# Attention's q, k and v transfers in 8-block transposes and one store of v per 512 tokens

## The chip, the cores and the metric

The kernel runs on one core of one Trainium2 chip. The metric is the device time of one execution in microseconds (us), as the median of three runs.

## The reference

One decoder layer over 2048 tokens of width 1024, with 8 heads of 64. One projection makes six streams; a gated short convolution and dilated attention run side by side on them; their outputs are normed, projected and added to x; a gated feed-forward part follows.

```python
h = rms_norm(x, g_mix[l])
z = h @ w_in[l]
u, gb, gc, q, k, v = jnp.split(z, splits, axis=-1)
y_conv = gb * short_conv(gc * u, conv_w[l])
q = rms_norm(q.reshape(B, S, N_HEADS, HEAD_DIM), g_q[l]) * (HEAD_DIM ** -0.5)
k = rms_norm(k.reshape(B, S, N_HEADS, HEAD_DIM), g_k[l])
v = v.reshape(B, S, N_HEADS, HEAD_DIM)
y_attn = dilated_mixture(q, k, v).reshape(B, S, D_ATTN)
mix = jnp.concatenate([rms_norm(y_conv, g_conv_out[l]), rms_norm(y_attn, g_attn_out[l])], axis=-1)
x = x + mix @ w_out[l]
h = rms_norm(x, g_ffn[l])
x = x + (jax.nn.silu(h @ w_gate[l]) * (h @ w_up[l])) @ w_down[l]
```

`dilated_mixture` lets every head attend in three branches of (window, dilation): (128, 1), (512, 4) and (2048, 16). In each, a query sees at most 129 keys at the branch's stride; the branches are summed with weights from their softmax denominators. Attention has no other positions.

## The kernel before

Products keep nearly full precision by splitting each operand in two halves of float16 (`h` and `l`) and adding three matmuls (L187 to L189).

**Stages.** `in_and_conv` norms x (`norm`, L251: 16 tiles of 128 tokens, each turned by two transposes into `self.x`), splits and spills the weights, and runs three of four convolution blocks (`conv_steps`). `attention_pairs` makes q, k and v of the first head pair alone (`qkv_steps(0)`). Then, for each of the four pairs `g`, the steps of `attn_steps(g)` alternate with steps of a filler: `qkv_steps(g + 1)` while there is a next pair, then `tail_steps` (the last convolution block and `out_a`, the first half of the output projection). `out_b` and `ffn` follow.

**What sets the order.** The code is recorded in program order, and a scheduler then orders every engine's instructions by its own estimate of when each is ready. Only edges like `issue_after` (L713) bind it. On the chip each engine runs its list in order: what waits holds up all that stands behind it. All large DMAs and all transposes stand in one such list, SyncE's (SP).

**`qkv_steps`** goes through the 2048 tokens in four steps of 512. In each, four matmul groups (128 tokens, 384 columns: q and k of two heads, v of two heads) are read out. v goes as two halves into `vs`, and is stored to DRAM (`d_v`, L466) after the second and the fourth group, for each head apart. DVE and POOL norm q and k. ACT and POOL then split them into `qkhl` (q of head 0 and 1 as halves, k's upper half twice) and `klz` (k's lower half beside zeros), L483 to L486. Six transposes of 4 blocks of 128 x 128 follow (L489 to L494): two into `qp`, two into `ka`, two into `kb` (called `kl` in the code). Two copies on DVE (L496) put `qp` into `qT` in token order.

**`attn_steps`** runs, for each of a pair's two heads, the branches in the order 1, 2, 0 (numbered from 0 as listed above): load v for the branch (`load_v`), score matmuls into `s` (L597, L598), DVE's mask and row minimum (L603), ACT's exponential (L608). Where the blocks have earlier keys, ACT and DVE make the halves `eh` (L618, L619; four buffers) and one transpose of 8 blocks turns them into `et` (L620). Where they have none (branch 2, and the first step of branch 1), the result goes to `sm` and TensorE transposes it (L613). Then come the AV matmuls into `av` (L626), and ACT copies `av` out (L629).

**Tiles.** The pool `qk` has three names, `qT`, `ka` and `kb`, with four buffers of 4 KB each per partition. They serve attention's `qT`, `ka` and `kl` (two buffers each for the two heads of a pair), and also the norm's halves, the convolution's `cu` and `w2`, and the tiles `ya`, `t`, `x1` and `xn` of the output projection. A tile takes whichever buffer of its name the scheduler finds free.

Of the kernel before, what the change touches and what calls it, by code (L numbers as in the profile page):

```python
# [8 lines left out]
F32 = mybir.dt.float32  # L9
# [8 lines left out]
P = 128  # L18
S = 2048
# [10 lines left out]
class Builder:  # L30
# [237 lines left out]
    def conv_steps(self, j, W, before=None, scratch=None):  # L268
# [3 lines left out]
        NC = 512  # L272
        prev = None
        for c in range(S // NC):
            if before:
# [20 lines left out]
            ups, u = yield from gemm(0)  # L296
            cu = own[:, 4:6].rearrange("p a b -> p (a b)") if own is not None else self.qk.tile([P, D], F32, name="ka")
            if c == 0:
# [9 lines left out]
            gb, u = yield from gemm(1)  # L308
            w2 = own[:, 2:4] if own is not None else self.qk.tile([P, 2, NC], F32, name="kb")
            y, s2 = w2[:, 0], w2[:, 1]  # L310
# [45 lines left out]
    def in_and_conv(self):  # L356
        tc, nc, A = self.tc, self.nc, self.A
        w_in, w_out = A["w_in"][0], A["w_out"][0]
        with ExitStack() as c:
# [23 lines left out]
            def norm(i, n):  # L383
                tags = 6 * ("nx_x",) + ("qT", "qT") + 8 * ("nx_x",)
                self.norm(i, [(self.qk if tg != "nx_x" else xp).tile([P, D], F32, name=tg) for tg in tags[i:i + n]],
                          [self.qk.tile([P, 2, D], F16, name=tg) for tg in ("ka", "ka", "ka", "qT")[i % 4:i % 4 + n]])
            spills = []
# [45 lines left out]
    def qkv_steps(self, g, st):  # L433
# [8 lines left out]
        qT = [self.qk.tile([P, S], F16, name="qT") for _ in range(2)]  # L442
        ka = [self.qk.tile([P, S], F16, name="ka") for _ in range(2)]
        kl = [self.qk.tile([P, S], F16, name="kb") for _ in range(2)]
        dv = self.d_v[g]
        for i in range(0, NT, 4):
            f = self.at.tile([P, 4, 4, HD], F32, name="qkf", bufs=2)
            for j in range(4):
                vs = self.vs[j // 2]

                t = slice(j, 4 * P, 4)
                xh, xl = self.x[i // 4]
                ps = self.psmm.tile([P, 512], F32, name="mm")
                yield from self.mm3_steps(ps[:, 0:384], lambda k: xh[:, k, t], lambda k: xl[:, k, t],
                                          lambda k: wh[:, k], lambda k: wl[:, k])
                if j == 0:
                    n = self.at.tile([P, 16, HD], F32, name="qkn")
                nc.scalar.activation(f[:, j].rearrange("p a b -> p (a b)"), ps[:, 0:256], AF.Copy, scale=u)
                nc.scalar.activation(n[:, 4 * j:4 * j + 4].rearrange("p a b -> p (a b)"), ps[:, 0:256], AF.Square, scale=u)
                pv = ps[:, 256:384].rearrange("p (h d) -> p h d", h=2)  # L460
                vh, vl = (vs[:, j % 2, :, x, 0:HD] for x in range(2))
                nc.scalar.activation(vh, pv, AF.Copy, scale=2.0 ** -20)
                nc.vector.scalar_tensor_tensor(vl, pv, 2.0 ** -20, vh, op0=ALU.mult, op1=ALU.subtract)  # L463
                if j % 2 == 1:
                    for h in range(2):
                        nc.sync.dma_start(dv[h, i * P:(i + 4) * P].rearrange("(p t) c -> p t c", t=4)[:, j - 1:j + 1],  # L466
                                          vs[:, :, h].rearrange("p t x d -> p t (x d)"))
            ff = f.rearrange("p a b d -> p (a b) d")
# [10 lines left out]

            hl = self.at.tile([P, 4, 4, 2, HD], F16, name="qkhl")  # L480
            for h in range(2):
                q, k = n4[:, :, h], n4[:, :, 2 + h]
                nc.scalar.copy(hl[:, h, :, 0], q)  # L483
                nc.scalar.copy(hl[:, 2 + h], k.unsqueeze(2).broadcast_to([P, 4, 2, HD]))
                nc.gpsimd.tensor_tensor(hl[:, h, :, 1], q, hl[:, h, :, 0], op=ALU.subtract)
                nc.gpsimd.tensor_tensor(self.klz[:, h, :, 0], k, hl[:, 2 + h, :, 0], op=ALU.subtract)  # L486


            four = [self.at.tile([P, 4, P], F16, name="qp", bufs=4) for _ in range(2)]  # L489
            for src, dsts in ((hl, (*four, *ka)), (self.klz, kl)):  # L490
                for n_, dst in enumerate(dsts):
                    self.transpose(dst if n_ < 2 and src is hl else
                                   dst[:, i * P:(i + 4) * P].rearrange("p (j t) -> p j t", j=4),
                                   src[:, n_].rearrange("p j x d -> p (j x d)"))  # L494
            for h in range(2):
                nc.vector.tensor_copy(qT[h][:, i * P:(i + 4) * P].rearrange("p (t j) -> p t j", j=4),  # L496
                                      four[h].rearrange("p j t -> p t j"))
            yield
        st.update(qT=qT, ka=ka, kl=kl)

    def attn_steps(self, g, st):
# [18 lines left out]
        for h, b in [(h, b) for h in range(2) for b in (1, 2, 0)]:  # L520
            qT, ka, kl = (st[x][h] for x in ("qT", "ka", "kl"))
            load_v(h, b)
# [39 lines left out]
            def keys(tl, u, prev):  # L562

                k = tl.rearrange("p (n j t) -> p n j t", n=4, j=4)
                n = u // 4
                if b == 0:
                    m = u % 4
                    k = k.rearrange("p n j (m t) -> p n m j t", m=4)
                    if prev and m == 0:
                        return [k[:, n - 1, 3], k[:, n, 0]]  # L570
                    return [k[:, n, m - prev:m + 1]]
                if b == 1:
                    return [k[:, n - prev:n + 1, u % 4]]
                return [k[:, :, u % 4, u // 4::4]]
# [5 lines left out]
            for u0 in (0, 8, 4, 12) if last and b == 0 else range(0, NT, 4):  # L580
# [3 lines left out]
                for us in (range(u0, u0 + 4),) if four else (range(u0, u0 + 2), range(u0 + 2, u0 + 4)):  # L584
# [14 lines left out]

                    sm = self.ep.tile([P, 512], F32, name="sm") if four else sp  # L600

# [56 lines left out]
    def attention_pairs(self):  # L658
# [29 lines left out]

        self.klz = self.at.tile([P, 2, 4, 2, HD], F16, name="klz")
        nc.gpsimd.memset(self.klz, 0.0)  # L690
        self.y7 = self.rows.tile([P, NT, HD], F32, name="y7")

        self.vs = [self.at.tile([P, 2, 2, 2, HD + 1], F16, name=f"vs{i}") for i in range(2)]
        for t in self.vs:
# [58 lines left out]
    def out_a(self, p):  # L753

        nc = self.nc
        mt = self.ma[:, p % 2]
        ya = self.qk.tile([P, 4, 2, P], F32, name="ka") if p < 2 else self.op.tile([P, 4, 2, P], F32, name="ya")
        for j in range(2):
# [6 lines left out]
        for j in range(2):  # L765
            i = p + 8 * j
            x1 = self.qk.tile([P, D], F32, name="kb" if p % 3 == 1 else "qT")
            nc.sync.dma_start(x1, self.A["x"][0][i * P:(i + 1) * P])
            t = self.qk.tile([P, 512], F32, name="ka") if p < 2 else self.op.tile([P, 512], F32, name="xt", bufs=2)

# [10 lines left out]
    def out_b(self):  # L781
        tc, nc, A = self.tc, self.nc, self.A
        with ExitStack() as c:
# [37 lines left out]
            def tiles(p, mt):  # L821

                t = self.big.tile([P, 4, 512], F32, name="b6")
                xs = []
                ss = op.tile([P, 2], F32, name="op_s2", bufs=2)
                for j in range(2):
# [8 lines left out]
                    nc.sync.dma_start(self.d_x1[rows], x1)  # L837
                    xn = self.qk.tile([P, D], F32, name="ka")
                    nc.scalar.activation(xn, x1, AF.Square, accum_out=ss[:, j:j + 1])
# [345 lines left out]
```

## Time and profile before

| | before |
|---|---|
| median of 3 runs | 2226.68 us (2224.04 to 2229.55) |
| profiled execution, its own time | 2224.36 us |
| its span, first to last instruction | 2222.6 us |
| mean granted TensorE clock | 0.975 |
| TensorE busy | 2081.2 us, 94% |
| VectorE (DVE), ScalarE (ACT), GpSimd (POOL) busy | 1453.5, 1030.2, 624.6 us |

In the rows below PE is TensorE's matmuls and PEld its weight loads, which overlap them. L489 is line 489 of the kernel. `out<-in` names the tiles that an instruction writes and reads. SPq rows are DMA issues on SyncE's queue: their time is how long the queue needs to issue, not how long the transfer runs. A wait names the engine that was idle, and what ended last before it went on. The clock is 1 at TensorE's upper level.

### The profile page before, as it was taken

What the parts mean: (1) busy time and instruction counts of PE and PEld (TensorE: products, weight loads), DVE (VectorE), ACT (ScalarE), POOL (GpSimd) and SP (SyncE); (2) the same over time, 40 slices, a digit from 0 to 9 for tenths busy, and PEclk for the clock granted to TensorE, in tenths of its full rate; (3) what the DMA queues carried; (4) which work ended last, traced back from release to release, by engine and by line L of the source; (5) the groups of instructions that cost most, each with busy time, mean ns of one, the idle gap of its engine ahead of it and who ended that gap; (6) DMA issues with size and microseconds to landing.
All of it is one profiled execution on the core that took longest, in us unless ns stands there. A gap on an engine that the chain in (4) does not pass through costs nothing.

```text
span 2222.6 us, 33037 instructions
## 1 busy us (share of the span) xinstructions
PE 2081.2 (94%) x11864; PEld 1080.7 (49%) x11864; DVE 1453.5 (65%) x3380; ACT 1030.2 (46%) x2134; POOL 624.6 (28%) x515
## 2 busy tenths in 40 slices
PE   4999999888888979989799999999999999999999
PEld 2344567666665644434344444444444444444444
DVE  6587446677766777884676767666666565555554
ACT  6343347666765756753343433343333343433341
POOL 0000133343343201230321112111211235555463
PEclk9999999999999989999899999999999999999999
DMA  9667368889999998889432332233223544252342
GB/s 248 159 199 256 98 123 148 176 159 180 178 168 190 210 210 259 238 215 259 150 119 95 109 100 91 91 105 109 86 90 104 194 169 161 65 194 58 114 142 95
DMA packets 570085, 339.66 MB, mean 153 GB/s; under 512 B 373312, under 2 KB 522816, under 8 KB 567488
## 3 DMA queue, kind: packets, MB, share of 16 engines
q1 hardware_dynamic: 564912, 337.46, 58.3%
q8 instruction: 93, 1.52, 0.3%
q10 hardware_dynamic: 5008, 0.08, 0.1%
q14 instruction: 72, 0.59, 0.1%
HBM read 161.24 MB, written 107.54 MB: 121 GB/s over the span
## 4 chain that ended last, share of the span: by engine, by line
PE 54%; DVE 3%; DMA 2%; SPq 1%; ACT 1%; issue 1%; DVEq 0%; ACTq 0%
PE ps L989 32%; PE ps L1107 18%; DVE hl L856 1%; SPq L195 1%; PE mm L187 1%; PE mm L188 1%; PE mm L189 1%; DMA wq<-d_a 1%; PE ps L187 1%; PE ps L188 1%; PE ps L189 1%; DVE w L900 1%; DMA b<-b 0%; DMA wq<-in_w_up_dram 0%; DMA hb<-d_h 0%
## 5 line engine op out<-in xcount | busy, mean ns | idle before, releaser
L989 PEld LDWEIGHTS <-w 128*128 128x128 f16 x3696 | 363.4, 98 | 470.1 <-issue 23.0
L989 PE MATMUL ps<-b,w 128*128 128x512 f16 x2112 | 467.5, 382 | 15.7 <-DMA b<-d_h 8.8
L1107 PE MATMUL ps<-b,w 128*128 128x512 f16 x1848 | 399.3, 379 | 0.9 <-DVE s L1125 0.8
L989 PE MATMUL ps<-hb,w 128*128 128x512 f16 x1584 | 350.7, 381 | 9.4 <-DVE s L995 8.3
L1107 PEld LDWEIGHTS <-w 128*128 128x128 f16 x1848 | 180.8, 98 | 219.2 <-issue 1.4
L882 POOL TENSOR_TENSOR t<-wq 128x512 f32<-128x512 f32 (+1 forms) x46 | 59.1, 1285 | 439.2 <-issue 205.8
L995 DVE TENSOR_TENSOR s<-ps,s 128x512 f32<-128x512 f32 x220 | 150.2, 683 | 41.9 <-PE ps L989 41.3
L187 PE MATMUL mm<-wq,b 128*128 128x384 f16 x512 | 172.0, 336 | 3.7 <-DVE vs L463 3.6
L188 PE MATMUL mm<-wq,b 128*128 128x384 f16 x512 | 171.9, 336 | 0.0
L189 PE MATMUL mm<-wq,b 128*128 128x384 f16 x512 | 171.5, 335 | 0.0
L1114 POOL TENSOR_TENSOR x<-x,s 128x512 f32<-128x512 f32 x72 | 103.1, 1433 | 186.3 <-DVE s L1125 128.8
L1115 DVE SCALAR_TENSOR_TENSOR x<-ps,a_u,x 128x512 f32<-128x512 f32 x96 | 71.9, 749 | 111.4 <-PE ps L1107 82.9
L608 ACT ACTIVATE s<-s,u 128x256 f32<-128x256 f32 (+1 forms) x224 | 97.2, 451 | 67.1 <-DVE u L603 49.8
L603 DVE CUSTOM_DVE_ANT_0 s<-s,mask,nkap 128x256 f32<-128x256 f32 (+1 forms) x224 | 103.8, 481 | 24.5 <-PE s L598 20.8
L626 PE MATMUL av<-v,et 128*128 128x65 f16 x1800 | 80.1, 197 | 41.3 <-DMA et<-eh 25.9
L188 PEld LDWEIGHTS <-b 128*128 128x128 f16 x768 | 84.5, 110 | 63.9 <-issue 15.2
L187 PEld LDWEIGHTS <-b 128*128 128x128 f16 x768 | 84.4, 110 | 62.6 <-issue 5.5
L189 PEld LDWEIGHTS <-b 128*128 128x128 f16 x768 | 84.2, 110 | 57.9 <-issue 5.1
L187 PE MATMUL cvx<-b,wq 128*128 128x512 f16 (+1 forms) x200 | 76.1, 384 | 29.5 <-ACT wq L145 25.0
L597 PE MATMUL s<-ka,qT 128*128 128x128 f16 (+1 forms) x408 | 92.5, 272 | 11.0 <-DVE eh L619 10.1
L626 PEld LDWEIGHTS <-et 128*128 128x128 f16 x1800 | 73.7, 100 | 59.3 <-DMA et<-eh 34.8
L619 DVE TENSOR_TENSOR eh<-s,eh 128x512 f16<-128x512 f32 (+1 forms) x112 | 75.3, 676 | 41.3 <-ACT eh L618 40.7
(301 smaller groups left out, 3750.9 us busy)
## 6 DMA issues: line engine op xcount, KB each, us to landing
d_a<-a SPq DMA_DIRECT2D x88, 256.0 KB, 2.0
d_wd<-w SPq DMA_DIRECT2D x77, 256.0 KB, 2.0
wq<-d_a SPq DMA_DIRECT2D x64, 256.0 KB, 4.2
b<-d_wd SPq DMA_DIRECT2D x14, 1024.0 KB, 6.5
wraw<-in_w_in_dram SPq DMA_DIRECT2D x24, 512.0 KB, 7.1
d_h<-hl SPq DMA_DIRECT2D x24, 512.0 KB, 3.8
wq<-in_w_gate_dram SPq DMA_DIRECT2D x22, 512.0 KB, 5.3
wq<-in_w_up_dram SPq DMA_DIRECT2D x22, 512.0 KB, 5.4
```

The costliest lines, as they stand in the source:

```text
L187: self.pe = mm(ps, lhsT=lh(k), rhs=rh(k), start=k == ks[0], stop=False)
L188: mm(ps, lhsT=lh(k), rhs=rl(k), start=False, stop=False)
L189: mm(ps, lhsT=ll(k), rhs=rh(k), start=False, stop=k == ks[-1])
L597: nc.tensor.matmul(o, lhsT=query(u), rhs=hi[x], start=True, stop=False)
L603: nc.vector.tensor_tensor_reduce(sm[:, at[u]], sp[:, at[u]], mask[:, P - P * has_prev(u):256], accum_out=Ub[:, u, HD + 1:HD + 2], op0=ALU.add,
L608: nc.scalar.activation(sm[:, at[u]], sm[:, at[u]], AF.Exp, scale=-1.0, bias=Ub[:, u, HD + 1:HD + 2])
L619: nc.vector.tensor_tensor(eh[:, w:2 * w], sm[:, 0:w], eh[:, 0:w], op=ALU.subtract)
L626: self.pe_av = nc.tensor.matmul(av[:, u - u0], lhsT=p_, rhs=v_, start=n_ == 0, stop=n_ == len(ops) - 1)
L989: nc.tensor.matmul(ps[self.BANK[n]], lhsT=w[:, x, k], rhs=b[:, y, k], start=first and k == 0 and q == 0, stop=k == 3 and q == 2, skip_grou ...
L995: nc.vector.tensor_tensor(t, x, y, op=ALU.add)
L1107: nc.tensor.matmul(ps[self.BANK[n]], lhsT=L[n][:, x, f], rhs=B[n][:, f, y], start=first and f == 0 and q == 0, stop=f == n_f - 1 and q == ...
L1114: nc.gpsimd.tensor_tensor(o, o, s_, op=ALU.add)
```

## The change

Three things are put together. First, `qkhl` gets all six pieces (q of two heads, k's upper half of two heads, k's lower half of two heads) as one fixed tile, `klz` goes, and three transposes of 8 blocks, each for both heads, take the place of six of 4. For that `ka` and `kl` of a pair become one tile of 8 KB each, laid out by 512 tokens and head, and `qp` one tile for both heads. Second, `vs` holds 512 tokens of two heads, and one DMA stores it after the fourth group. Third, `ka` and `kb` of the pool `qk` have two buffers of 8 KB instead of four of 4 KB, and every other user of these names takes two of its tiles as one: the norm's halves (now in `ka` and `kb`, before in `ka` and `qT`), `cu` and `w2` of two convolution steps, `ya` with both `t`, and `x1` and `xn` of two token tiles. `sm` has two buffers instead of three.

```diff
@@ conv_steps
+        two = {}
+
+        def pair(c, name):
+
+            if name not in two or j < 3 and c % 2 == 0:
+                two[name] = self.qk.tile([P, 2, D], F32, name=name, bufs=2)
+            return two[name][:, c % 2]
...
-            cu = own[:, 4:6].rearrange("p a b -> p (a b)") if own is not None else self.qk.tile([P, D], F32, name="ka")
+            cu = own[:, 4:6].rearrange("p a b -> p (a b)") if own is not None else pair(c, "ka")
...
-            w2 = own[:, 2:4] if own is not None else self.qk.tile([P, 2, NC], F32, name="kb")
+            w2 = own[:, 2:4] if own is not None else pair(c, "kb").rearrange("p (a b) -> p a b", a=2)
@@ in_and_conv, norm
-                          [self.qk.tile([P, 2, D], F16, name=tg) for tg in ("ka", "ka", "ka", "qT")[i % 4:i % 4 + n]])
+                          [t[:, j] for tg in ("ka", "kb")[i % 4 // 2:(i % 4 + n) // 2]
+                           for t in (self.qk.tile([P, 2, 2, D], F16, name=tg, bufs=2),) for j in range(2)])
@@ qkv_steps
-        ka = [self.qk.tile([P, S], F16, name="ka") for _ in range(2)]
-        kl = [self.qk.tile([P, S], F16, name="kb") for _ in range(2)]
+
+        ka, kl = (self.qk.tile([P, 4, 2, 512], F16, name=nm, bufs=2) for nm in ("ka", "kb"))
...
-                vs = self.vs[j // 2]
+                vs = self.vs[i // 4 % 2]
...
-                vh, vl = (vs[:, j % 2, :, x, 0:HD] for x in range(2))
+                vh, vl = (vs[:, :, j, x, 0:HD] for x in range(2))
...
-                if j % 2 == 1:
-                    for h in range(2):
-                        nc.sync.dma_start(dv[h, i * P:(i + 4) * P].rearrange("(p t) c -> p t c", t=4)[:, j - 1:j + 1],
-                                          vs[:, :, h].rearrange("p t x d -> p t (x d)"))
+                if j == 3:
+                    nc.sync.dma_start(dv[:, i * P:(i + 4) * P].rearrange("h (p t) c -> p h (t c)", t=4),
+                                      vs.rearrange("p h t x d -> p h (t x d)"))
...
-            hl = self.at.tile([P, 4, 4, 2, HD], F16, name="qkhl")
+            hl = self.qkhl
...
-                nc.gpsimd.tensor_tensor(self.klz[:, h, :, 0], k, hl[:, 2 + h, :, 0], op=ALU.subtract)
+                nc.gpsimd.tensor_tensor(hl[:, 4 + h, :, 0], k, hl[:, 2 + h, :, 0], op=ALU.subtract)
...
-            four = [self.at.tile([P, 4, P], F16, name="qp", bufs=4) for _ in range(2)]
-            for src, dsts in ((hl, (*four, *ka)), (self.klz, kl)):
-                for n_, dst in enumerate(dsts):
-                    self.transpose(dst if n_ < 2 and src is hl else
-                                   dst[:, i * P:(i + 4) * P].rearrange("p (j t) -> p j t", j=4),
-                                   src[:, n_].rearrange("p j x d -> p (j x d)"))
+            qp = self.at.tile([P, 2, 4, P], F16, name="qp", bufs=2)
+            for n_, dst in enumerate((qp, ka[:, i // 4].rearrange("p h (j t) -> p h j t", j=4),
+                                      kl[:, i // 4].rearrange("p h (j t) -> p h j t", j=4))):
+                self.transpose(dst.rearrange("p h j t -> p (h j) t"),
+                               hl[:, 2 * n_:2 * n_ + 2].rearrange("p h j x d -> p (h j x d)"))
@@ attn_steps
-                    sm = self.ep.tile([P, 512], F32, name="sm") if four else sp
+                    sm = self.ep.tile([P, 512], F32, name="sm", bufs=2) if four else sp
@@ attention_pairs
-        self.klz = self.at.tile([P, 2, 4, 2, HD], F16, name="klz")
-        nc.gpsimd.memset(self.klz, 0.0)
+        self.qkhl = self.at.tile([P, 6, 4, 2, HD], F16, name="qkhl")
+        nc.gpsimd.memset(self.qkhl[:, 4:6, :, 1], 0.0)
...
-        self.vs = [self.at.tile([P, 2, 2, 2, HD + 1], F16, name=f"vs{i}") for i in range(2)]
+        self.vs = [self.at.tile([P, 2, 4, 2, HD + 1], F16, name=f"vs{i}") for i in range(2)]
@@ out_a
-        ya = self.qk.tile([P, 4, 2, P], F32, name="ka") if p < 2 else self.op.tile([P, 4, 2, P], F32, name="ya")
+        if p < 2:
+            tk = self.qk.tile([P, 2, 2, 512], F32, name="ka", bufs=2)
+            ya = tk[:, 0].rearrange("p a (b c) -> p (a b) c", c=2 * P).rearrange("p k (j t) -> p k j t", j=2)
+        else:
+            ya = self.op.tile([P, 4, 2, P], F32, name="ya")
+        xk = self.qk.tile([P, 2, D], F32, name="kb", bufs=2) if p % 3 == 1 else None
...
-            x1 = self.qk.tile([P, D], F32, name="kb" if p % 3 == 1 else "qT")
+            x1 = self.qk.tile([P, D], F32, name="qT") if xk is None else xk[:, j]
...
-            t = self.qk.tile([P, 512], F32, name="ka") if p < 2 else self.op.tile([P, 512], F32, name="xt", bufs=2)
+            t = tk[:, 1, j] if p < 2 else self.op.tile([P, 512], F32, name="xt", bufs=2)
@@ out_b, tiles
+                xk = self.qk.tile([P, 2, D], F32, name="ka", bufs=2)
...
-                    xn = self.qk.tile([P, D], F32, name="ka")
+                    xn = xk[:, j]
```

The scheduler orders the new program anew. SP's queue, in the second pair's attention while q, k and v of the third pair are made. The names: `et` is the probabilities, `qp`, `ka` and `kb` are q and k, `d_v` is v in DRAM, `v` the tile it is loaded to. Before:

```order
L195 DMA_TRANSPOSE et<-eh 128x8x128 x3
L195 DMA_TRANSPOSE qp<-qkhl 128x4x128 x2
L195 DMA_TRANSPOSE et<-eh 128x8x128
L195 DMA_TRANSPOSE ka<-qkhl 128x4x128 x2
L195 DMA_TRANSPOSE kb<-klz 128x4x128
L195 DMA_TRANSPOSE et<-eh 128x8x128
L195 DMA_TRANSPOSE kb<-klz 128x4x128
L195 DMA_TRANSPOSE et<-eh 128x8x128
L466 DMA d_v_63<-vs_2143 128x2x130 x2
L195 DMA_TRANSPOSE et<-eh 128x8x128
L515 DMA v<-d_v_62 128x2080
L195 DMA_TRANSPOSE et<-eh 128x8x128
```

The same place now, with the `qkhl` rows for both heads and `d_v` written once:

```order
L195 DMA_TRANSPOSE et<-eh 128x8x128
L518 DMA v<-d_v_62 128x4x520
L195 DMA_TRANSPOSE qp<-qkhl 128x8x128
L195 DMA_TRANSPOSE ka<-qkhl 128x8x128
L195 DMA_TRANSPOSE et<-eh 128x8x128 x2
L195 DMA_TRANSPOSE kb<-qkhl 128x8x128
L195 DMA_TRANSPOSE et<-eh 128x8x128 x2
L521 DMA v<-d_v_62 128x2080
L195 DMA_TRANSPOSE et<-eh 128x8x128
L473 DMA d_v_63<-vs_2123 128x2x520
L195 DMA_TRANSPOSE et<-eh 128x8x128 x3
```

Six issues for q and k became three, spread among the same `et` issues, and two pairs of stores became one store.

VectorE's (DVE) list in the last filler for q, k and v, the second step of the fourth pair. `L496` (now `L502`) copies q out of `qp`, `L619` (now `L626`) is the subtraction that makes `eh`, `L603` (now `L610`) the mask. Before:

```order
L463 SCALAR_TENSOR_TENSOR vs_2143<-mm,vs_2143 128x2x64
L496 COPY qT<-qp 128x512
L619 TENSOR_TENSOR eh<-s,eh 128x512
L603 ISA s,u<-s,mask,nkap 128x256
L603 ISA u 128x1
L496 COPY qT<-qp 128x512
L619 TENSOR_TENSOR eh<-s,eh 128x512
L615 TENSOR_TENSOR et<-pt,et 128x512
L463 SCALAR_TENSOR_TENSOR vs_2144<-mm,vs_2144 128x2x64
L619 TENSOR_TENSOR eh<-s,eh 128x512
```

Now:

```order
L610 ISA s,u<-s,mask,nkap 128x256
L610 ISA u 128x1
L502 COPY qT<-qp 128x512 x2
L610 ISA s,u<-s,mask,nkap 128x256
L610 ISA u 128x1
L626 TENSOR_TENSOR eh<-s,eh 128x512
L622 TENSOR_TENSOR et<-pt,et 128x512
L471 SCALAR_TENSOR_TENSOR vs_2123<-mm,vs_2123 128x2x64
L626 TENSOR_TENSOR eh<-s,eh 128x512 x2
```

The two copies stood apart with a subtraction and a mask between them. They now follow each other, and the subtractions of `eh` come behind both.

## Rows read from the trace of the kernel before

**Rows 1.** The page, part 1: busy us, share of the span, instructions.

```profile
PE 2081.2 (94%) x11864; PEld 1080.7 (49%) x11864; DVE 1453.5 (65%) x3380; ACT 1030.2 (46%) x2134; POOL 624.6 (28%) x515
```

**Rows 2.** Stages: window, length, busy per engine (instructions), clock, DMA share, GB/s.

```profile
310.00:700.00 390.00, 347.86 (x3323) 260.52 (x3322) 273.68 (x999) 255.25 (x683) 141.53 (x112) 0.96 0.90 169
...
250.00:310.00 60.00, 58.77 (x364) 40.80 (x362) 21.66 (x90) 25.02 (x67) 17.88 (x21) 0.98 0.27 54
```

**Rows 3.** TensorE's waits, 310 to 700 us: total us, times, longest us.

```profile
PE av L626 <- DMA et<-eh: 15.2, 8, 4.4
PE s L597 <- DVE eh L619: 9.3, 10, 2.9
PE av L626 <- ACT u L629: 7.0, 7, 3.0
PE av L626 <- DMA v<-d_v: 2.9, 1, 2.9
...
PE pt L613 <- ACT sm L608: 1.1, 2, 1.0
```

**Rows 4.** SP's queue in time, 484 to 522 us: start, us, issue.

```profile
492.56 3.38 SPq L466 DMA_DIRECT2D d_v<-vs  x4
...
497.28 8.36 SPq L195 DMA_TRANSPOSE et<-eh  x3
505.73 2.54 SPq L195 DMA_TRANSPOSE qp<-qkhl  x2
...
509.67 3.41 SPq L195 DMA_TRANSPOSE ka<-qkhl  x2
513.18 1.21 SPq L195 DMA_TRANSPOSE kb<-klz  x1
...
515.84 1.23 SPq L195 DMA_TRANSPOSE kb<-klz  x1
...
518.48 1.10 SPq L466 DMA_DIRECT2D d_v<-vs  x2
```

**Rows 5.** Three shorter windows, columns as in rows 2.

```profile
484.00:522.00 38.00, 30.19 (x271) 21.75 (x269) 28.04 (x87) 21.40 (x58) 15.30 (x11) 0.91 0.82 159
422.00:446.00 24.00, 18.39 (x145) 12.24 (x144) 9.95 (x36) 13.26 (x35) 5.69 (x6) 0.79 0.95 183
...
608.00:650.00 42.00, 33.95 (x356) 25.86 (x355) 30.08 (x103) 25.07 (x65) 20.58 (x14) 0.96 1.04 177
```

**Rows 6.** By line, whole program: ns min/median/max, first and last start.

```profile
L195 SPq DMA_TRANSPOSE et<-eh x112: 1209/1264/5631, 310.6 to 812.4; - x112
L195 SPq DMA_TRANSPOSE qp<-qkhl x32: 1189/1223/2400, 268.3 to 681.4; - x32
L195 SPq DMA_TRANSPOSE ka<-qkhl x32: 1188/1258/4035, 270.9 to 686.4; - x32
L195 SPq DMA_TRANSPOSE kb<-klz x32: 1199/1218/2742, 273.5 to 695.0; - x32
...
L466 SPq DMA_DIRECT2D d_v<-vs x64: 360/472/6006, 253.3 to 671.7; - x64
...
L485 POOL TENSOR_TENSOR qkhl<-qkn,qkhl x32: 667/672/683, 267.6 to 680.0; 128x256 f16<-128x256 f32 x32
```

**Rows 7.** DMA, 310 to 700 us: packets, MB, share; issues, median us to landing.

```profile
q1 hardware_dynamic: 199443, 65.32, 89.1%
...
d_v<-vs SPq DMA_DIRECT2D x51, 65.0 KB, 4.8
...
et<-eh SPq DMA_TRANSPOSE x84, 3.8
qp<-qkhl SPq DMA_TRANSPOSE x26, 3.3
```

**Rows 8.** One of TensorE's waits, 0 to 250 us.

```profile
PE cvx L187 <- ACT ka L301: 2.6, 1, 2.6
```

**Rows 9.** One of VectorE's waits, 310 to 700 us.

```profile
DVE qT L496 <- DMA qp<-qkhl: 16.2, 10, 4.3
```

More of the change, by code (lines that the diff above doesn't have):

```diff
@@ L485, in qkv_steps @@
                 nc.gpsimd.tensor_tensor(hl[:, h, :, 1], q, hl[:, h, :, 0], op=ALU.subtract)
-                nc.gpsimd.tensor_tensor(self.klz[:, h, :, 0], k, hl[:, 2 + h, :, 0], op=ALU.subtract)
-            four = [self.at.tile([P, 4, P], F16, name="qp", bufs=4) for _ in range(2)]
-            for src, dsts in ((hl, (*four, *ka)), (self.klz, kl)):
-                for n_, dst in enumerate(dsts):
-                    self.transpose(dst if n_ < 2 and src is hl else
-                                   dst[:, i * P:(i + 4) * P].rearrange("p (j t) -> p j t", j=4),
-                                   src[:, n_].rearrange("p j x d -> p (j x d)"))
+                nc.gpsimd.tensor_tensor(hl[:, 4 + h, :, 0], k, hl[:, 2 + h, :, 0], op=ALU.subtract)
[4 more added lines that the diff above has]
+                               hl[:, 2 * n_:2 * n_ + 2].rearrange("p h j x d -> p (h j x d)"))
             for h in range(2):
                 nc.vector.tensor_copy(qT[h][:, i * P:(i + 4) * P].rearrange("p (t j) -> p t j", j=4),
-                                      four[h].rearrange("p j t -> p t j"))
+                                      qp[:, h].rearrange("p j t -> p t j"))
             yield
@@ L520, in attn_steps @@
         for h, b in [(h, b) for h in range(2) for b in (1, 2, 0)]:
-            qT, ka, kl = (st[x][h] for x in ("qT", "ka", "kl"))
+            qT = st["qT"][h]
+            ka, kl = (st[x][:, :, h] for x in ("ka", "kl"))
             load_v(h, b)
@@ L562, in keys @@
             def keys(tl, u, prev):
-                k = tl.rearrange("p (n j t) -> p n j t", n=4, j=4)
+                k = tl.rearrange("p n (j t) -> p n j t", j=4)
                 n = u // 4
```

## The prediction

> **What bounds the kernel now.** I read the page first, then the trace cut by stage, then who waits for whom in the one stage that holds most of the changed work.
>
> TensorE is busy 94% of the span [rows 1]. The stages tell where the rest is. The feed-forward part, after 1100 us, is one chain of matmuls, and the change doesn't touch it. From 0 to 250 us (projections and convolution) and from 830 to 1100 us (output projection) the change moves only tiles. From 250 to 310 us the first head pair's q, k and v are made alone: TensorE is busy 58.77 of 60 us. From 310 to 700 us attention runs, with the next pair's q, k and v as filler between its steps: TensorE 347.86 of 390 us, clock 0.96, DMA share 0.90 [rows 2]. From 700 to 830 us attention runs on with other filler, and nothing of the changed work is left in it.
>
> So the question is what the 42.1 us of idle TensorE in 310 to 700 are, and what its clock costs there. The waits [rows 3] name the four largest: AV products wait 15.2 us for the transposed probabilities (`et<-eh`), scores wait 9.3 us for DVE's subtraction that makes `eh`, AV waits 7.0 us for ACT's copy out of its only accumulator, and once 2.9 us for a load of v. The second and third follow from the first: `eh` has four buffers, which come free when a transpose has read them, and the accumulator comes free when the late AV products are done. With the load of v, which follows the stores of v through the same queue, that makes 34.4 us behind SP's queue.
>
> Is it the queue that makes `et` late? In 484 to 522 us SP issues one DMA behind the other. Between the `et` transposes stand two `qp`, two `ka`, two `kb` and six stores of v [rows 4], and a block of probabilities that is ready stands behind them. TensorE is busy 30.19 us of these 38, at clock 0.91 [rows 5].
>
> **The change part by part.** *Transposes.* The program has 96 transposes of 4 blocks (32 each of `qp`, `ka`, `kb`), and gets 48 of 8. To issue 4 blocks takes SP 1223, 1258 and 1218 ns in the median; `et<-eh`, which is 8 blocks, takes 1264 ns [rows 6]. So issue time goes by the instruction, not by its blocks. In 310 to 700 us there are 26 of each kind [rows 7]: 78 x 1.23 = 95.9 us become 39 x 1.26 = 49.1 us, 46.8 us off SP. The bytes through the DMA engines stay.
>
> *Stores of v.* Four of 65 KB per 512 tokens become one of 260 KB. An issue takes 472 ns in the median [rows 6]; 51 in the stretch [rows 7] become 13, so 38 x 0.47 = 17.9 us go. The runs in SBUF grow from 260 to 1040 bytes by the code's shapes. The mean packet of the stretch takes 0.891 x 390 us x 16 / 199443 = 27.9 ns [rows 7]; 51 stores are 13056 packets, 22.8 us on 16 engines. Afterwards 3328 packets cost between 5.8 us (the same time each) and 22.8 us (four times each). So the DMA engines get back 0 to 17 us; no row shows the new store. I take the middle, 8 us, and count it inside the next term.
>
> Together 64.7 us leave SP's queue in 390 us, 5.0 us in each of the 13 steps of 512 tokens.
>
> *What of that reaches TensorE.* The bounds are 0 and the 34.4 us. In 484 to 522 us the queue gets lighter by 8.39 - 3 x 1.26 = 4.6 us for transposes and 4.48 - 1.5 x 0.47 = 3.8 us for stores [rows 4]: 8.4 us against 7.8 us of idle TensorE, which would be all of it. But in the same rows three `et` issues take 8.36 us instead of 3.8: there the DMA engines hold the queue up, and fused transposes don't lift that. This excess of 4.6 us is over half of the idle time. I take half of the bound: **17 us**.
>
> *Clock.* 0.96 over 390 us means that some 31 us ran at 1.2 instead of 2.4 GHz, which costs at most 15.6 us. It is 0.79 in 422 to 446 us, where 5.6 of 24 us are idle, and 0.96 in 608 to 650 us, where 8.1 of 42 are [rows 5]: it falls where the waits lie close together. With half the waits gone I take half: **7 us**, bounds 0 and 15.6.
>
> *What waits longer.* A fused `qp` needs both heads' subtraction on POOL, the second 0.67 us after the first [rows 6]; the first of the old pair could go one subtraction earlier. Whatever stands behind it in SP's queue, `et` above all, waits with it. 13 x 0.67 = 8.7 us more at SP is the upper end and none the lower, since the queue ahead is shorter; a quarter of it at TensorE is **2 us** lost. I take a quarter because the relief of 64.7 us is worth 17 by the same count. The store of v goes after the fourth token block instead of after the second and the fourth. Its wait hides behind the whole attention of the pair before, except for the first pair, where the load of v cost 2.9 us: that can move by 3 us either way.
>
> *Edits at no cost.* `sm` has two buffers instead of three: TensorE's transposes wait 1.1 us for it in two waits [rows 3], since the filler sets their pace. Without that cover it is 0.55 us for each of the 40 steps that use it, 22 us. `ka` and `kl` as one tile for two heads: two sets remain, this pair's and the next one's. `qkhl` is one buffer, as it was. Tiles of 8 KB tie two uses together in the convolution and the output projection: in the convolution TensorE waited 2.6 us for `ka` once [rows 8], which could go or double, 3 us either way. In 250 to 310 us TensorE is full, and nothing is won.
>
> Sum: -17 - 7 + 2 = -22 us on the profiled execution's 2224.4 us (span 2222.6), which is 2202 us. That execution lies 2.3 us below the median of the runs, so I put the median at **2203 us**.
>
> One page speaks against the largest term. The Trainium skill (DMA: Bandwidth & Descriptors, section "Issuing engines are not separate DMA queues") says that the sequencer's time to start a DMA is usually small beside the DMA itself. Here it isn't: a transpose costs SP 1.26 us of the 3.8 us to its landing, and the queue had no pause [rows 4, 6, 7]. By the page's sentence issue time would be worth nothing, and the first rival's time would follow.
>
> **Rivals.** *The DMA engines are the bound.* For: their share is 0.90 over the stretch and 1.04 in 608 to 650 us [rows 2, 5], the transposes move what they moved, and three `et` in 8.36 us are held up by the engines. Then only the packets of the v store count: 0 to 17 us of DMA time, up to half of it at TensorE: 0 to 8 us, 2219 to 2227 us, mostly no change. Against: the share is 0.82 in 484 to 522 us, where TensorE waits as large a part of the time as in 608 to 650 us.
>
> *DVE stands behind the fused `qp`: slower.* DVE copies `qp` to `qT` in its own order. The two copies stood apart, with masks and an `eh` subtraction between them; now they stand together, with the `eh` subtractions behind both. DVE waited 16.2 us for `qp` in 10 waits, 4.3 us at the longest [rows 9]. The fused one is issued a subtraction later (0.67 us) and lands as 8 blocks do (3.8 instead of 3.3 us [rows 7]). If DVE reaches the pair early and stands 4.3 us in each of the 13 steps, that is 56 us, 40 more than now. DVE is busy 273.68 of 390 us, so I let half be absorbed; 20 us reach TensorE, with some 8 us of clock, and the queue's relief is worth nothing because `eh` itself is late: 2224 + 28 = 2252 us. With part of the relief kept it is 2231 to 2255 us, 2242 in the middle. It decides from where that wait passes 16 + 2 x 24 = 64 us. Against: `qp` itself waits in SP's queue now (at 505.73 it stands behind three `et` in 8.36 us), and that gets shorter.
>
> *The change doesn't do what it says:* an issue of 8 blocks that costs as much as two of 4. The `et` row speaks against it. About 2225.
>
> **How the numbers follow.** A measurement of this kernel tells 0.3%, 6.7 us, from no change. Forecast: 0.60, 2178 to 2219 us (with all of the 34.4 and 15.6 us gone it would be 2174). DMA bound: 0.22, nearly all between 2220 and 2233. DVE: 0.15, nearly all above 2233. No effect: 0.03. So faster 0.62, same 0.22, slower 0.16. The range from 2178 to 2236 leaves out the last of the gain (0.06) and most of the DVE case (0.11).
>
> **What would show it.** Right: in attention SP pauses between issues, AV's wait for `et` falls from 15.2 us to about 8, the scores' wait for `eh` and AV's for ACT's copy fall with it, the clock rises to about 0.98, and attention up to the last of the q, k, v work is some 20 us shorter. DMA bound: SP's issues get longer, or SP pauses and the wait for `et` stays. DVE: its wait for `qp` is over 50 us. Wrong altogether if the time moves before 250 or after 830 us by more than 5 us.

## The result and the profile after

The changed kernel takes 2200.65 us (2197.79 to 2202.29, five runs) beside 2228.4 us (2224.04 to 2233.89, five runs) of the kernel before: a ratio of 0.9877, interval 0.9861 to 0.9893. Timed once more on another occasion it was 0.9865 (0.9843 to 0.9887). The profiled execution after took 2202.29 us, its span is 2200.5 us and its mean granted clock 0.981. The medians lie 27.8 us apart and the two profiled executions 22.1 us: what follows from the traces accounts for the 22.1 alone.

The page's first part, as [rows 1]:

```profile
PE 2070.1 (94%) x11864; PEld 1076.9 (49%) x11864; DVE 1454.9 (66%) x3380; ACT 1027.3 (47%) x2134; POOL 629.6 (29%) x515
```

TensorE does the same 11864 matmuls in 11.1 us less, and it is idle 11.0 us less: together the 22.1 us between the spans (2222.6 and 2200.5 us). Where they went is read from windows that end at the same work in both kernels: the first score matmul, the last q, k, v matmul, the last AV product, the first feed-forward matmul. Columns as in [rows 2]. Before:

```profile
0.00:287.10 287.10, 244.71 (x1185) 123.27 (x1186) 185.04 (x447) 122.86 (x239) 26.00 (x45) 0.96 0.70 187
287.10:667.90 380.80, 337.89 (x3195) 257.17 (x3194) 262.11 (x965) 248.75 (x670) 137.04 (x108) 0.96 0.87 165
667.90:820.00 152.10, 132.91 (x1223) 85.58 (x1221) 107.50 (x406) 89.19 (x223) 32.76 (x23) 0.91 0.99 209
820.00:985.10 165.10, 158.00 (x721) 70.62 (x721) 131.17 (x257) 105.60 (x193) 36.67 (x36) 0.99 0.81 233
985.10:2222.60 1237.50, 1207.65 (x5545) 544.07 (x5543) 767.68 (x1308) 463.75 (x812) 392.15 (x304) 0.99 0.39 124
```

After:

```profile
0.00:284.60 284.60, 243.41 (x1184) 123.38 (x1185) 186.25 (x447) 122.32 (x238) 26.20 (x45) 0.98 0.72 189
284.60:650.70 366.10, 333.11 (x3216) 257.27 (x3214) 267.30 (x966) 248.98 (x672) 138.52 (x108) 0.97 0.89 172
650.70:798.60 147.90, 131.26 (x1222) 82.94 (x1220) 108.40 (x406) 88.94 (x225) 33.77 (x23) 0.97 1.00 213
798.60:961.10 162.50, 154.70 (x705) 69.30 (x702) 126.60 (x258) 106.99 (x195) 37.85 (x35) 0.97 0.83 237
961.10:2200.50 1239.40, 1207.58 (x5545) 544.00 (x5543) 766.39 (x1306) 460.04 (x806) 393.21 (x304) 0.99 0.40 123
```

The stage in which attention runs beside the next pair's q, k and v gives 14.7 us: 4.8 us of TensorE's busy time, and 9.9 us of its idle time (42.9 to 33.0 us). The front gives 2.5, the rest of attention 4.2 and the output projection 2.6 us; the feed-forward part takes 1.9 us more. The changed kernel's other profiled execution had 371.2 us in the second stage, a gain of 9.6 us instead of 14.7: a stage is known to some 5 us.

TensorE's waits in that stage after, 285 to 651 us (all four of [rows 3] lie in the same stage before):

```profile
PE av L633 <- DMA et<-eh: 9.2, 10, 2.2
PE s L604 <- DVE eh L626: 7.3, 4, 4.2
PE mm L187 <- DVE vs L471: 6.5, 5, 1.9
PE av L633 <- DMA v<-d_v: 4.9, 1, 4.9
PE av L633 <- ACT u L636: 3.1, 2, 1.8
...
PE pt L620 <- ACT sm L615: 0.5, 1, 0.5
```

The four groups that the prediction put behind SP's queue fall from 34.4 to 24.5 us, by 9.9 us (to 28.3 us in the other profiled execution). Two waits grew: matmuls for q, k and v wait for DVE's read of v, 6.5 us (3.1 before), and AV for the load of v, 4.9 us (2.9).

SP's queue in time, 478 to 520 us, the place that answers to [rows 4]:

```profile
491.73 1.23 SPq L195 DMA_TRANSPOSE qp<-qkhl  x1
493.06 2.47 SPq L195 DMA_TRANSPOSE ka<-qkhl  x1
495.64 2.63 SPq L195 DMA_TRANSPOSE et<-eh  x2
498.36 2.50 SPq L195 DMA_TRANSPOSE kb<-qkhl  x1
502.43 2.61 SPq L195 DMA_TRANSPOSE et<-eh  x2
...
507.09 0.54 SPq L473 DMA_DIRECT2D d_v<-vs  x1
511.50 6.22 SPq L195 DMA_TRANSPOSE et<-eh  x3
```

The queue pauses here (500.9 to 502.4, 507.6 to 511.5 us), where in [rows 4] it did not. Pauses as such are not new: in the whole stage those of over 0.5 us add up to 48 us of 380.8 before and to 111 us of 366.1 after. SP issues in 81% of the stage's time before and in 65% after. By line, whole program, as [rows 6], and the new rows of [rows 7], 310 to 700 us:

```profile
L195 SPq DMA_TRANSPOSE et<-eh x112: 1231/1275/5880, 306.8 to 788.4; - x112
...
L195 SPq DMA_TRANSPOSE ka<-qkhl x16: 1232/1318/3063, 266.7 to 670.4; - x16
L195 SPq DMA_TRANSPOSE qp<-qkhl x16: 1232/1286/2366, 268.0 to 664.0; - x16
L195 SPq DMA_TRANSPOSE kb<-qkhl x16: 1232/1290/2496, 269.4 to 672.5; - x16
L473 SPq DMA_DIRECT2D d_v<-vs x16: 359/488/2917, 259.5 to 654.0; - x16
```

```profile
d_v<-vs SPq DMA_DIRECT2D x13, 260.0 KB, 4.5
et<-eh SPq DMA_TRANSPOSE x89, 4.2
qp<-qkhl SPq DMA_TRANSPOSE x13, 3.4
```

8 blocks are issued in 1.29 to 1.32 us in the median, 4 blocks in 1.22 to 1.26 before, as `et` said. Summed over all issues that begin in 310 to 650 us, SP issues for 283 us before and 227 after. From the end of DVE's `eh` to the issue of its transpose it is 4.9 us in the mean before and 1.9 after, in the same 340 us. Below this time is called the lateness of the issue: what a block of probabilities loses behind other issues of SP's queue, a wait for a free `et` tile included.

### The profile page after: what moved, and what is told of

It reads as the page before. It is cut to its first block, busy times and chain, and to the rows that moved or that the text cites. A ratio compares the mean times of both kernels' runs of the same rounds, so it can differ in the third digit from the quotient of the medians.

```text
span 2200.5 us, 32856 instructions
## 1 busy us (share of the span) xinstructions
PE 2070.1 (94%) x11864; PEld 1076.9 (49%) x11864; DVE 1454.9 (66%) x3380; ACT 1027.3 (47%) x2134; POOL 629.6 (29%) x515
## 5 line engine op out<-in xcount | busy, mean ns | idle before, releaser
L895 POOL TENSOR_TENSOR t<-wq 128x512 f32<-128x512 f32 (+1 forms) x46 | 59.2, 1286 | 440.5 <-issue 207.7
L610 DVE CUSTOM_DVE_ANT_0 s<-s,mask,nkap 128x256 f32<-128x256 f32 (+1 forms) x224 | 104.3, 482 | 19.2 <-PE s L605 13.4
L912 ACT CAST w<-t 128x512 f16<-128x512 f32 x88 | 53.6, 615 | 108.6 <-PE ps L1002 86.9
L1107 ACT CAST w<-t 128x512 f16<-128x512 f32 (+1 forms) x96 | 53.7, 580 | 92.2 <-PE ps L1120 75.1
```

What stands on the lines that cost most here:

```text
L610: nc.vector.tensor_tensor_reduce(sm[:, at[u]], sp[:, at[u]], mask[:, P - P * has_prev(u):256], accum_out=Ub[:, u, HD + 1:HD + 2], op0=ALU.add,
```

## The experiments

Three theories. **Q**: SP's time counts, spent on issuing. **D**: the DMA engines' time counts, spent on packets. **T**: the new tiles and the new order that comes with them count. In every kernel the scheduler orders all engines anew, so a difference of a few us between two kernels can be order alone. Each kernel computes all that the changed one does.

**The change in parts.** From the changed kernel one part is undone at a time, or both. The six transposes again, from the new tiles:

```
-                self.transpose(dst.rearrange("p h j t -> p (h j) t"),
-                               hl[:, 2 * n_:2 * n_ + 2].rearrange("p h j x d -> p (h j x d)"))
+                for h in range(2):
+                    self.transpose(dst[:, h], hl[:, 2 * n_ + h].rearrange("p j x d -> p (j x d)"))
```

The four stores of v again (`vs` as before):

```
-                if j == 3:
-                    nc.sync.dma_start(dv[:, i * P:(i + 4) * P].rearrange("h (p t) c -> p h (t c)", t=4),
-                                      vs.rearrange("p h t x d -> p h (t x d)"))
+                if j % 2 == 1:
+                    for h in range(2):
+                        nc.sync.dma_start(dv[h, i * P:(i + 4) * P].rearrange("(p t) c -> p t c", t=4)[:, j - 1:j + 1],
+                                          vs[:, :, h].rearrange("p t x d -> p t (x d)"))
```

Transposes fused, four stores:

> The changed kernel with v stored as before: twice per 512 tokens for each head, in 65 KB pieces. Theory Q (SP's issue time is what counts): transposes are 46.8 of the 64.7 us that leave SP's queue, so about 70% of the gain of 27 us stays, 2207 to 2213 us. Theory D (DMA engine time is what counts): only the v store's longer packets helped, so the gain is gone, 2224 to 2230 us. Theory T (the 8 KB tiles and the new order they lead to): the whole gain stays, 2198 to 2204 us.

Six transposes, one store:

> The changed kernel with six transposes of 4 blocks per 512 tokens, out of the same tiles; v stored once. Q: the stores are 17.9 of 64.7 us of queue time, so about 8 us of gain, 2217 to 2223 us. D: nearly the whole gain, 2198 to 2206 us. T: the whole gain, 2198 to 2204 us.

Both undone, so that the tiles alone are new:

> The changed kernel's tiles of 8 KB and its two sm buffers, but six transposes of 4 blocks and the four small stores of v. Q: nothing is left of the gain, 2222 to 2234 us. D: the same, 2222 to 2234 us. T: the whole gain, 2198 to 2204 us.

The kernel before with `bufs=2` for `sm` and nothing else:

> The kernel before with two sm buffers instead of three, nothing else. All theories: the filler covers it, 2224 to 2232 us, and TensorE's wait for sm stays at 1 to 2 us. If the cover is thinner than the prediction said, up to 22 us more, 2240 to 2250 us.

Measured, as ratios to the kernel before: transposes 0.9938 (0.9920 to 0.9955), store 0.9938 (0.9917 to 0.9958), tiles alone 0.9973 (0.9959 to 0.9987), two `sm` 0.9995 (0.9984 to 1.0007). The kernel before took 2219.4 us beside these, so the times foretold are compared as ratios. Q had the transposes alone (0.991 to 0.994); no theory had the store or the tiles, and T, which gave the tiles the whole gain, falls. The two transfers are worth the same, some 8 us each beyond the tiles. The third buffer of `sm` was worth nothing. The lateness of the issue follows Q: 4.4 us with the tiles alone, 3.9 with the store, 3.2 with the transposes, 1.9 with both.

The tiles alone were run again:

> The change's tiles with the six transposes and the four stores of before, once more (0.9973, interval 0.9959 to 0.9987, when first timed; its trace showed attention as long as before, 533.3 us from the first score to the last AV product against 532.9, and the time missing after it). Theory of the tiles (8 KB tiles free the output projection): again 0.997, and the stretch between the last AV product and the first feed-forward matmul again near 156 us (165 before). Theory of chance (the tiles do nothing): 0.999 to 1.001.

It gave 0.9981 (0.9969 to 0.9993): a gain of 4 to 6 us that both runs show. Where it lies isn't settled. The stretch from the last AV product to the first feed-forward matmul was short in both traces (156.1 and 158.0 us, 165.1 before), but in the second attention took as much longer: from the first score to the first feed-forward matmul they have 689.4 and 697.7 us, the kernel before 698.0.

Tiles (0.9977 in the middle), transposes and store add up to 0.990; the whole change gave 0.987. The missing 6 us are no more than the uncertainty of the sum itself (0.003, from the intervals of its parts), so whether the parts help one another isn't settled.

**The store: instructions or packets.** Two kernels store v with one instruction per head, two for the change's one. In one of them `vs` is laid out by token first, as before, which makes runs of 260 bytes:

```
-                vh, vl = (vs[:, :, j, x, 0:HD] for x in range(2))
+                vh, vl = (vs[:, j, :, x, 0:HD] for x in range(2))
...
+                    for h in range(2):
+                        nc.sync.dma_start(dv[h, i * P:(i + 4) * P].rearrange("(p t) c -> p t c", t=4),
+                                          vs[:, :, h].rearrange("p t x d -> p t (x d)"))
```

In the other the change's tile and its runs of 1040 bytes stay:

```
+                    for h in range(2):
+                        nc.sync.dma_start(dv[h, i * P:(i + 4) * P].rearrange("(p t) c -> p (t c)", t=4),
+                                          vs[:, h].rearrange("p t x d -> p (t x d)"))
```

> The changed kernel once more, beside the three kernels below on one chip, so that they can be compared with it. Both theories: a ratio to the kernel before of about 0.988, as when it was first timed. If the parts add up as they were timed apart (tiles alone 0.9973, transposes on top 0.9938, store on top 0.9938) it would be 0.990.

> v stored by one instruction per head and 512 tokens (two instead of the change's one), from a tile with the order of before, so that the runs in SBUF are 260 bytes again: 1024 packets per 512 tokens as in the kernel before. Theory Q (only the time of issuing on SP's queue counts): 16 more issues of 0.5 to 0.7 us than the changed kernel, +1 to +2 us, and the same as with long runs. Theory D (the DMA engines' time for the small packets counts: the share of 310 to 650 us fell from 0.90 to 0.87 where only the store was fused, some 12 us): most of the store's gain is gone, +5 to +8 us on the changed kernel, about 2207 us or 0.9935.

> The partner of the kernel with two stores and short runs: again one instruction per head and 512 tokens, but with the change's tile, runs of 1040 bytes, 256 packets per 512 tokens. Theory Q: as with short runs, +1 to +2 us on the changed kernel. Theory D: +0 to +1 us on the changed kernel, and 5 us or more under its partner.

Measured: the changed kernel 0.9865 (0.9843 to 0.9887), short runs 0.9921 (0.9902 to 0.9940), long runs 0.9860 (0.9838 to 0.9882). One more instruction per store costs nothing that can be measured; the short runs cost 0.6%, 13 us. The short runs' store by line, and its issues and those of `et`, 310 to 700 us:

```profile
L474 SPq DMA_DIRECT2D d_v<-vs x32: 513/627/2951, 261.6 to 669.3; - x32
```

```profile
d_v<-vs SPq DMA_DIRECT2D x26, 130.0 KB, 6.3
et<-eh SPq DMA_TRANSPOSE x85, 4.2
```

The long runs':

```profile
L474 SPq DMA_DIRECT2D d_v<-vs x32: 319/425/2900, 261.8 to 658.2; - x32
```

```profile
d_v<-vs SPq DMA_DIRECT2D x26, 130.0 KB, 3.3
et<-eh SPq DMA_TRANSPOSE x89, 3.5
```

With short runs the store lands after 6.3 us instead of 3.3, and the `et` transposes after 4.2 instead of 3.5. By the trace's packets (310 to 650 us, loads of v among them) one of 260 bytes takes 24 ns of an engine and one of 1040 bytes 55 ns, so the stretch's stores are 13312 x 24 / 16 = 20.0 us against 3328 x 55 / 16 = 11.4 us on the 16 engines. In 250 to 310 us, where stores alone have these sizes, it is 19 and 48 ns: 15.8 against 10.0 us. So the length of the runs counts, and Q, which had the two alike, fails as it was put. But the pair doesn't separate the theories: an issue with short runs also takes 0.2 us longer, and SP issues for 237.5 us in 310 to 650 us instead of 228.3. Nor is a later `et` the path: from the end of `eh` to the landing it is 7.0 and 6.9 us in the mean, because with short runs the issue is less late (2.5 instead of 3.0 us). By which way the 13 us arise stays open.

**SP's time.** Small DMAs that nobody waits for are put behind the three transposes; they write 64 bytes each to a scratch tensor. First eight per 512 tokens that read a constant:

```
+                for x in range(3 * n_, (3, 6, 8)[n_]):
+                    nc.sync.dma_start(self.d_n[g][2 * i + x:2 * i + x + 1], self.kgain[0:1, 0:16])
```

> The changed kernel with eight more DMAs of 64 bytes behind the three transposes of each 512 tokens (three, three and two), which nobody waits for: eight issues of about 0.47 us are 3.8 us of SP's time per 512 tokens, as much as the three transposes that the change saves, and almost no time of the DMA engines. Theory Q: what the fused transposes gave is gone, +6 to +8 us, ratio about 0.991 to 0.992, AV waits for the transposed probabilities some 8 us more. Theory D: within 2 us of the changed kernel, and SP's pauses get shorter.

Ratio 0.9868 (0.9845 to 0.9890), which is D's forecast. But the trace shows half of them elsewhere:

```profile
L503 SPq DMA_DIRECT2D d_n<-gk x128: 214/250/1257, 256.2 to 418.6; - x128
```

Since they wait for nothing, the scheduler put 67 of the 128 ahead of 310 us, and they are cheaper than I took them for. The other 61 take 18 us of SP in 310 to 419 us. There they raise the lateness of the issue from 1.8 to 3.3 us, and no time is lost that can be measured: this much the queue could bear. In the next two they read what the transposes read:

```
+                for x in range(6 * n_, (6, 12, 16)[n_]):
+                    nc.sync.dma_start(self.d_n[g][4 * i + x:4 * i + x + 1], hl[0:1, 2 * n_, 0, 0, 0:32])
```

> The changed kernel with sixteen more DMAs of 64 bytes per 512 tokens, six, six and four behind the three transposes. They read the tile that the transposes read, so that they can't be issued earlier than these (the eight of the run before read a constant and went out ahead of attention, up to 410 us). A small issue took 0.25 to 0.29 us there: 16 x 0.27 = 4.3 us of SP's queue per 512 tokens, somewhat more than the three issues of 1.26 us that the fused transposes save. Theory Q (what the fused transposes save is SP's time): +6 to +8 us on the changed kernel, ratio about 0.990, AV's wait for the transposed probabilities up by some 8 us. Theory D (DMA engines): within 2 us of the changed kernel, ratio 0.986 to 0.988.

> The same with forty small DMAs per 512 tokens (fourteen, fourteen and twelve): 10.8 us of SP's queue in each of the 13 steps of 26 us in attention, 140 us in all, more than twice of all that the change took off the queue (64.7 us by the prediction). Theory Q: the queue is fuller than in the kernel before, so slower than that: ratio 1.00 or more. Theory D: the queue has pauses of about a third of the time and takes most of it; up to +8 us, ratio 0.987 to 0.991.

Sixteen: 1.0029 (1.0017 to 1.0040), 0.3% slower than the kernel before, where Q gave about 0.990 and D 0.986 to 0.988. Forty: 1.0680 (1.0654 to 1.0706). The sixteen by line, its stage from the first score to the last q, k, v matmul, and TensorE's waits there:

```profile
L503 SPq DMA_DIRECT2D d_n<-qkhl x256: 214/251/1904, 266.7 to 709.2; - x128
```

```profile
286.70:674.30 387.60, 342.02 (x3247) 262.48 (x3245) 267.30 (x984) 252.91 (x679) 137.46 (x108) 0.95 0.81 160
```

```profile
PE av L636 <- DMA et<-eh: 19.2, 16, 2.5
PE s L607 <- DVE eh L629: 17.4, 11, 4.5
```

The DMA share falls from 0.89 to 0.81 while the stage grows from 366.1 to 387.6 us and TensorE waits twice as long for `et` and `eh` (36.6 instead of 16.5 us). In the stage SP issues for 311 us, as in the kernel before (310), and the lateness of the issue is 5.8 us in 310 to 650 us (4.9 before, 1.9 in the changed kernel). So DMA engines that are kept busy don't set this time; what SP has to issue does. None of an engine's waits there names the small DMAs or their tile's release. The price: by the trace the 256 issues are 91 us of SP, and the ratio is 0.0164 above the changed kernel's (0.9865), 36 us: 0.4 us for each us of SP. Of the forty, with a window of attention and AV's wait in 285 to 980 us:

```profile
L503 SPq DMA_DIRECT2D d_n<-qkhl x640: 214/250/1437, 266.9 to 847.1; - x160
```

```profile
310.00:800.00 490.00, 352.20 (x3166) 261.35 (x3165) 270.24 (x959) 253.69 (x667) 132.68 (x103) 0.83 0.63 125
```

```profile
PE av L636 <- DMA et<-eh: 86.4, 19, 16.9
```

The 640 issues are 188 us of SP, and cost 0.0815, 181 us: nearly one for one. But not because the queue is full: SP issues for 385 of the stage's 509 us (76%; 80% with sixteen, 81% before) and pauses for up to 13 us. The issue of `et` is 15.1 us late in the mean in 310 to 650 us, and the whole chain waits for it: AV waits 86.4 us, and the clock falls to 0.83. In part it is the tile: POOL and ACT wait 9.8 us for the small DMAs to release `qkhl`. So the price isn't the busy time of the queue alone, and it has no fixed rate: nothing to measure for 18 us early in attention, 0.4 for 91 us, nearly 1 for 188 us. D, which gave the forty 0.987 to 0.991, falls here; Q gave them 1.00 or more, and was too mild for the sixteen.

This shows that SP's issuing is enough to lose the whole gain. It doesn't show that all that the fused transposes gave was SP's time: they also save the engines some 6 us of small packets (last section), and no run takes that apart.

The sentence of the Trainium skill that the prediction weighed (DMA: Bandwidth & Descriptors, section "Issuing engines are not separate DMA queues": the time to initiate a DMA is usually small) does not fit this case: DMAs of 64 bytes, whose packets take 0.1 to 0.2 us of the engines' mean time in 310 to 650 us, cost 36 us by their issuing, and 181 us together with the tile that they hold.

**Less on SP, by another engine.** The store of v and the two stores of the attention result are issued by ACT (three times `nc.sync` becomes `nc.scalar`).

> A try at a better version: the stores of v and of the attention result to DRAM are issued by ACT instead of SP, 23 issues of 0.5 to 0.8 us less on SP in 310 to 650 us (some 15 us), the same bytes and packets. Theory Q: -2 to -4 us on the changed kernel. Theory D: no change, or up to +3 us, since ACT's order gets 23 more waits for DVE.

0.9936 (0.9917 to 0.9955): 13 to 16 us slower than the changed kernel (0.9877 and 0.9865), which neither theory had. SP issues for 210 us in 310 to 650 us instead of 227, and the lateness of the issue is 1.8 us instead of 1.9, but TensorE's waits in the stage are:

```profile
PE av L633 <- DMA et<-eh: 20.1, 16, 2.8
PE av L633 <- DMA v<-d_v: 6.0, 2, 3.4
PE s L604 <- DVE eh L626: 5.9, 4, 4.4
```

AV waits longer for `et` than in the changed kernel (9.2 us), though the queue is lighter. The transposes aren't slower: from the end of `eh` to the landing it is 6.0 us in the mean, 6.2 in the changed kernel. So the loss lies outside SP's queue; where, the rows don't say, and it stays open. The Trainium skill (Perfetto Trace Analysis, section "DMA Optimizations") says that where descriptor generation is the bottleneck, balancing DMAs over the engines that can issue them may help; here it did not. No version tried beats the changed kernel by more than the measurement tells: two stores with long runs are level with it.

## Why the prediction was right, point by point

The forecast was 2203 us, the result 2200.65. The sum came out near; its terms were not all right. By its own figures the median should have been 2202.4 + 2.3 = 2204.7 us, not 2203. The gain foretold is 22 us; the profiled executions show 22.1, the medians 27.8, and no trace shows where the difference of 6 us lies.

- **The bound.** Right: SP's queue makes `et` late. The lateness of the issue (4.9 to 1.9 us, and 5.8 and 15.1 with small DMAs) shows it. The pauses were a weak sign: the "queue had no pause" holds for the 38 us of [rows 4], not for the stage, where it paused for 48 us before and 111 after.
- **Issue time per instruction.** Right: 1286, 1318 and 1290 ns for 8 blocks. For 340 us the 64.7 us of relief in 390 are 56.4; SP issued for 283 - 227 = 56 us less.
- **What reaches TensorE.** The mis-sized step: half of 34.4 us, 17 us, was taken for this stage; 9.9 us came (waits of 24.5 us left), and 6.1 us in the other profiled execution. Attention up to the last q, k, v matmul got 14.7 us shorter, not some 20. AV's wait for `et` fell to 9.2 us, near the 8 foretold, but the scores' wait for `eh` only from 9.3 to 7.3 us, and the load of v went up by 2 us. AV's wait for ACT's copy fell with it, 7.0 to 3.1 us. The excess of slow `et` issues did stay: three take 6.22 us at 511.50. That the engines hold them up isn't shown: their share is 0.67 in these 6.22 us, 1.02 in the 8.36 us before.
- **Clock.** 7 us taken, 4.8 us of busy time came in the stage, 0.97 instead of 0.98 (0.96 in the other profiled execution). Over the program busy time fell by 11.1 us.
- **What the sum left at nothing.** 2.5 us before the first score, 4.2 in the rest of attention and 2.6 in the output projection made up for it: 9.3 us, against 9.3 us that the stage gave less than the 24 of its two terms. The 2 us put down as lost are about the 1.9 us that the feed-forward part took more, for which the prediction had no reason. So the closeness of the total is partly luck. The tiles alone were worth 4 to 6 us, where I had 0 with 3 either way.
- **The store.** Its relief of the engines was taken as 8 us. The packets give 13056 x 24 / 16 = 19.6 us for 51 stores before, less 11.4 after: 8.2 us (5.5 by the 19 and 48 ns of the stores alone). But I counted its worth by its issues on SP, 28% of the relief, and it was worth as much as the transposes; the pair with short and long runs shows that the length of its runs counts. How much of that is the DMA rival's engine time, 0 to 8 us at TensorE, stays open.
- **The fused `qp`.** DVE doesn't stand behind it, so the second rival is out. Its wait, 310 to 700 us, against [rows 9]:

```profile
DVE qT L502 <- DMA qp<-qkhl: 15.4, 8, 6.2
```

  It lands after 3.4 us, not the 3.8 that I took from `et`. The 2 us charged for `et` behind a `qp` that waits for both heads can't be seen apart.
- **Edits at no cost.** Two `sm`: right, 0.5 us of waits, and no time in the kernel before. The convolution's `ka`: the first q, k, v matmul moved from 238.9 to 239.9 us, within the bound.
- **The places named as wrong.** The first q, k, v matmul before 250 us moved by 1.0 us; after the last AV product the two stages changed by -2.6 and +1.9 us. Neither passes 5 us.

## What to carry to other kernels

Price a DMA queue twice: by instructions in its issuer's time, and by packets in the engines' time, and fuse where one edit saves both. Don't take a queue's busy share for its price: 81% busy, it was the bound, and a us more of issuing cost from nothing to nearly a whole us by where it stood. Measure how long what the critical engine waits for stands in the queue (4.9 us before, 1.9 after). Compare stages that end at the same work, not at the same time, before putting a gain in a place.

## What the runs showed that I had not expected

- The cheapest DMA issue on SP takes 0.25 us in the median (64 bytes), a store of v 0.43 us with long and 0.63 us with short runs (two per 512 tokens), a transpose 1.22 us for 4 blocks and 1.29 for 8.
- A packet of 1040 bytes takes 2.3 times as long as one of 260 (55 against 24 ns, loads among them), four times the bytes.
- In 310 to 650 us the 4-byte packets take 9.3 us of the engines' mean time before and 3.1 after: some 80 of them last over 0.3 us before, and 4 after. With the fused transposes alone it is 3.5 us. What they wait for the trace doesn't tell.
